# Weight rows of 512 columns kept even columns first, odd ones behind, and read back in turn

## The chip, the core and the metric

The kernel runs on one core of one Trainium2 chip, as one program in one launch. The metric is the device time of one execution in microseconds (us). TensorE is called PE in the profile, its loading of the stationary operand PEld, VectorE is DVE, ScalarE is ACT, GpSimd POOL, and SP is the engine that issues most DMAs.

## What is computed

The reference is a trunk of two layers over one sequence of 256 tokens with 1024 channels, in float32. Cut to what matters here:

```python
def _token_mixer(xn, w_in, w_pool, pool_scale, w_a, w_b, w_o, rel_bias):
    u, q, k, v, g_pool, g_attn = jnp.split(xn @ w_in, SPLITS, axis=-1)
    ...
    merged = jax.nn.sigmoid(g_pool) * (pool_out @ w_a) + jax.nn.sigmoid(g_attn) * (attn_out @ w_b)
    return merged @ w_o

def _conv_ffn(xn, w_up, conv_w, conv_b, w_down):
    a, gval = jnp.split(xn @ w_up, 2, axis=-1)
    a = lax.conv_general_dilated(a, conv_w[:, None, :], ...) + conv_b
    return (jax.nn.gelu(a) * gval) @ w_down

def reference(x, ...):
    h = x
    for layer in range(DEPTH):
        h = h + _token_mixer(_rmsnorm(h, norm1[layer]), w_in[layer], ...)
        h = h + _conv_ffn(_rmsnorm(h, norm2[layer]), w_up[layer], ...)
    return _rmsnorm(h, norm_f)
```

Nearly all arithmetic is in the products with the weights `w_in` (1024 x 7680 a layer), `w_a`, `w_b`, `w_o`, `w_up` (1024 x 5632) and `w_down` (2816 x 1024). Each weight is used for 256 tokens only, so all of them pass from memory through the chip once.

## The kernel before, in words

**Two parts of every number.** The matrix unit is fed with float32r operands, which keep fewer bits than float32. So each float32 number is split into a high part (float32r) and a low part (what is left). A product of activations with weights is then three products: high with high, high with low, low with high, all added up in one PSUM tile.

**Weights.** The class `Weights` streams them. A load is one DMA of 1 MB from SP into a tile `raw` of 128 partitions x 2048 columns of float32 (three such buffers). A load is cut into two pieces of 128 x 1024 columns. For each piece, `open_next` gives two instructions: ACT copies the piece into `wh` with a cast to float32r (L191), and DVE subtracts that copy from the raw piece and writes `wl` (L192). There are five buffers each of `wh` and `wl` (some pieces use other tiles: `m2`, `ybig`, `at2`, `v1`), and the splitting runs three or more pieces ahead of the products. In the first layer's first eight pieces the split also multiplies by the norm's gain, 512 columns at a time (L199 on ACT, L200 on DVE).

**Products by rows.** Here the activations are the stationary operand (128 channels x 128 tokens, loaded into the array), and the weights stream past as the moving operand, 512 columns wide, into a PSUM tile of 128 tokens x 512 output columns. Three helpers do this:

- `v_sum` (called by `by_rows` and for the values): six products of a weight piece that holds two rows of 512 columns (L667). It serves `w_in`, `w_a`, `w_b` and `w_up`.
- `residual_mm` with its inner function `one` and `row_mm` (L564, L565, L566): weight pieces of one row of 1024 columns, read in slices of 512 columns, and near the end of a layer in some slices of 256. It serves `w_o` and `w_down`.
- `product` in `values_of_x` (L789): the first 96 products of the first layer.

**Products by channels.** For some queries and keys (`proj`, L536 and L538) and for the pool projections (`chunk_mm`, L528 to L530) the weights are the stationary operand and the activations move. These pieces have rows of 128 or 256 columns.

**Order.** The program runs in one stream on PE; every stage waits only for its piece of weights and for the activations of the stage before. The vector engines split weights ahead of PE, and between the splits they take results out of PSUM, build the attention's softmax, the convolution and the gelu. Every `wh` and `wl` buffer is handed back when the products that read it are done; ACT's next cast into that buffer waits for that.

The changed functions, and what calls them:

Of the kernel before, what the change touches and what calls it, by code (L numbers as in the profile page):

```python
# [75 lines left out]
def _edge_table():  # L76

    rows = []
    for w in WINDOWS:
        h = w // 2  # L80
        left = [w / (i + h) for i in range(h)]
        right = [w / (S - i + h) for i in range(S - h + 1, S)]
        rows.append(left + right + [1.0] * (16 - w + 1))
    return np.asarray(rows, np.float32).reshape(1, 64)


class Weights:
# [82 lines left out]
    def open_next(self):  # L170


        nc, i = self.nc, self.n_split
        n, cut, shape, slot = self.pieces[i]
        if slot is None:
            self.live.add(i)
            h, l = (
                self.pool.tile([P, *shape], F32R, tag=tag, bufs=self.BUFS, name=f"{tag}{i}")
                for tag in ("wh", "wl")
            )  # L180
        else:
            tag, part, of = (*slot, 0, 1)[:3]
            if part == 0:
                self.shared = self.idle.tile([P, of, 2, *shape], F32R, tag=tag, name=f"{tag}{i}")
            h, l = self.shared[:, part, 0], self.shared[:, part, 1]
        src = cut(self.raw[n])
        self.split[i] = (h, l)
        self.n_split += 1
        if i >= self.n_scaled:
            return [(  # L190
                lambda: nc.scalar.copy(out=h, in_=src),  # L191
                lambda: nc.vector.tensor_sub(out=l, in0=src, in1=h.bitcast(F32)),  # L192
            )]

        def scaled(j):
            k = i // 2 * shape[0] + j
            g = self.gains[:, k : k + 1]
            return (
                lambda: nc.scalar.activation(h[:, j], src[:, j], AF.Copy, scale=g),  # L199
                lambda: nc.vector.scalar_tensor_tensor(  # L200
                    out=l[:, j], in0=src[:, j], scalar=g, in1=h[:, j].bitcast(F32),
                    op0=ALU.mult, op1=ALU.subtract,
                ),
            )

        return [scaled(j) for j in range(shape[0])]
# [15 lines left out]
def encoder(ctx, tc, x, w_in, w_pool, pool_scale, w_a, w_b, w_o, norm1, norm2, w_up, conv_w,  # L222
# [20 lines left out]
    def rows(w, r0, n=2, c0=0, width=1024, tag=None, pieces=2):  # L243

        src = w[r0 : r0 + n * P, c0 : c0 + width].rearrange("(k p) c -> p k c", p=P)
        h = n // pieces
        return W.add(
            src, (n, width), [((lambda t, j=j: t[:, j * h : (j + 1) * h, :]), (h, width)) for j in range(pieces)],
            tag,
        )  # L250

    for l in range(DEPTH):
        if l == 0:
            slots = (("m2", 0, 2), ("m2", 1, 2), ("ybig",), ("at2",))
            for j in range(2):
                kept = rows(w_in[l], j * 512, 4, C_V, 512)
# [18 lines left out]
        for c in PAIRS:  # L275
            q = cols(w_in[l], C_Q + c * 256)
            k = cols(w_in[l], C_K + c * 256)
# [19 lines left out]
        for kind, n in ORDER.split():  # L297
            n = int(n)
# [4 lines left out]
            for j in range(2):  # L303
                if kind == "d":
                    W.use(rows(w_down[l], (4 * n + 2 * j) * P))
                elif kind == "r":
                    src = w_up[l][j * 512 : (j + 1) * 512].rearrange("(k p) c -> p k c", p=P)
                    c0 = (4 * n * P, 4 * n * P + DFF)
# [9 lines left out]
                else:  # L318
                    p = rows(w_up[l], j * 512, 4, (kind == "g") * DFF + 4 * n * P, 512)
# [4 lines left out]
    h = const.tile([P, 2, D], F32, name="h")  # L324
# [195 lines left out]
    def flush():  # L520

        while later:
            later.pop(0)()
# [38 lines left out]
    def row_mm(ps, ah, al, wh, wl, first, last):  # L562

        nc.tensor.matmul(ps, ah, wh, start=first, stop=False)  # L564
        nc.tensor.matmul(ps, ah, wl, start=False, stop=False)  # L565
        nc.tensor.matmul(ps, al, wh, start=False, stop=last)  # L566

    def residual_mm(parts, n, done, hold=4, fill=None, ahead=0, seeded=False):

        ps = [[acc.tile([P, 512], F32, tag="acc", name="res_ps") for _ in range(2)] for _ in range(2)]

        def one(part, ps_, t, cc, start, stop):
            ah, al, wh, wl = part
            row_mm(ps_, ah[:, t], al[:, t], wh[:, 0, cc], wl[:, 0, cc], start, stop)

        held = []
        for k in range(n):  # L580
            ah, al = parts(k)
            i, (wh, wl) = W.get(W.LOOK + ahead * (k >= n - hold - 2))
            flush()
            part = (ah, al, wh, wl)
            if k < n - hold:
                for t in range(2):
                    for c in range(2):
                        one(part, ps[t][c], t, slice(c * 512, c * 512 + 512), k == 0, False)
                W.free(i)
            else:  # L590
                held.append((i, part))
            yield
        then, half = None, None
        seed = None
        if seeded:
            one_r = sm.tile([P, P], F32R, tag="u", name="one_r")
            nc.scalar.copy(out=one_r, in_=ident)
        for t in range(2):
            segments = SEGMENTS[t]
            if t and seeded:  # L600
                segments = segments[1], segments[0], segments[2]
            for m, cc in enumerate(segments):
                c, c0 = divmod(cc.start, 512)
                res = ps[t][c][:, c0 : c0 + cc.stop - cc.start]
                if c0:

                    if not seed:
                        nc.vector.tensor_add(out=h[:, t, cc], in0=res, in1=h[:, t, cc])
                    res = mmp.tile([P, cc.stop - cc.start], F32, tag="mm", name="res2_ps")
                for j, (i, part) in enumerate(held):  # L610
                    one(part, res, t, cc, c0 != 0 and j == 0, j == hold - 1)
                    if c0 and j == 1:
                        for more in seed or ():
                            nc.tensor.matmul(res, one_r, more, start=False, stop=False)
                if half:
                    run(half)
                    half = None
                if then and m:
                    half = then()
                    next(half)  # L620
                    then = None
                then = done(t, m, cc, res, c0 != 0 and seeded) or then
                if t and seeded and m == 0:
                    rest = slice(768, D)
                    hi, lo = seed = [sm.tile([P, 256], F32R, tag="us", name="seed") for _ in range(2)]
                    nc.vector.tensor_add(out=h[:, t, rest], in0=ps[t][1][:, 256:], in1=h[:, t, rest])
                    nc.scalar.copy(out=hi, in_=h[:, t, rest])
                    nc.vector.tensor_sub(out=lo, in0=h[:, t, rest], in1=hi.bitcast(F32))
        if half:
            run(half)  # L630
        rest = fill() if fill else None
        half = then()
        next(half)
        if rest:
            rest()
        run(half)
        for i, _ in held:
            W.free(i)

    def run(gen):  # L640
        for _ in gen:
            pass
# [16 lines left out]
    def v_tile():  # L659
        return acc.tile([P, 512], F32, tag="acc", name="v_ps")  # L660

    def v_sum(ps, x2, t, n, piece, of=4):

        _, (wh, wl) = piece
        passes = [(0, wh, 0), (0, wl, 0), (1, wh, 0), (0, wh, 1), (0, wl, 1), (1, wh, 1)]
        for m, (part, w, j) in enumerate(passes):
            nc.tensor.matmul(  # L667
                ps, x2[:, 2 * n + j, part, t, :], w[:, j, :], start=(n + m == 0),
                stop=(n == of - 1 and m == 5),
            )  # L670

# [48 lines left out]
    def values_of_x(keep_values):  # L720
# [49 lines left out]
        x2 = two_parts("x", "x2")  # L770
        ps = [[v_tile() for _ in range(2)] for _ in range(2)]
# [14 lines left out]
        def product(k, g, t, kind):  # L786
            wh, wl = W.split[pieces[k // 2 * 2, g]]
            a, w = {"hh": (xuh, wh), "lh": (xul, wh), "hl": (xuh, wl)}[kind]
            return nc.tensor.matmul(  # L789
                ps[g][t], a[:, k, t, :], w[:, k % 2, :], start=k == 0 and kind == "hh",  # L790
                stop=k == KD - 1 and kind == "hl",
            )

# [110 lines left out]
    for l in range(DEPTH):  # L904
# [21 lines left out]
        if l == 0:  # L926
            with tc.manual_schedule():
                x2 = values_of_x(keep_values)
        else:
            for g in range(2):  # L930
                held = begun[0] if g == 0 else [W.get() for _ in range(4)]
                for t in range(2):
                    if g + t == 0:
                        ps = begun[1]
                    else:
                        ps = v_tile()
# [264 lines left out]
        for c in PAIRS:  # L1201
            for n in range(4):
                src, rest = (halves(a) for a in proj(x2))
# [27 lines left out]
        ps = by_rows(x2, 4, step)  # L1231
# [14 lines left out]
        for n, cc in enumerate(HALVES):  # L1246
            ps = by_rows(x2, 4, step)
# [67 lines left out]
        x2 = two_parts("x", "x2")  # L1315
# [150 lines left out]
        for kind, n in ORDER.split():  # L1466
# [9 lines left out]
            if (kind, n) == ("a", "0"):  # L1476
                held, ps = entry
                ps = [ps, v_tile()]
# [6 lines left out]
            else:  # L1485
                ps = by_rows(x2, 4, unit, W.LOOK + 1)
            n = int(n)
# [3 lines left out]
        if l + 1 < DEPTH:  # L1491
            x2 = two_parts("x", "x2")
# [34 lines left out]
```

## Time and profile before

| what | value |
|---|---|
| time, median of three runs | 857.28 us (857.15 to 857.35) |
| the profiled execution's own time | 857.48 us |
| its span, first to last instruction | 855.7 us |
| granted PE clock, mean | 0.999 |
| PE busy | 848.6 us, 4030 products |
| PEld busy | 711.5 us |
| DVE busy | 648.8 us |
| ACT busy | 477.3 us |
| POOL busy | 20.7 us |
| read from HBM | 160.65 MB |

The durations of products in the profile overlap: a product of 512 columns is listed with about 389 ns, but the next one starts long before those are over, and the ends are modelled. How long PE really takes for a product is therefore read from the distance between starts, as a stretch of the chain or of the timeline shows it. "f32" in a product's row is the size of its operands; they are float32r where the code says so. Names such as `rows_ps<-wh,x` give the output tile and the two inputs.

### The profile page before, as it was taken

The page shows a single profiled execution, that of the slowest core. Times are in us where ns is not written, and L with a number is a line of the kernel's source. Part 1 is how long each engine was busy: PE and PEld are TensorE (multiplying, and loading weights), DVE is VectorE, ACT ScalarE, POOL GpSimd, SP SyncE. Part 2 cuts the span into 40 slices and gives each one's busy share as a digit, 9 for nine tenths or more (in the row PEclk, how much of TensorE's full clock was granted, in tenths as well). Part 3 has the DMA queues.
Part 4 walks back from the last instruction along what each step waited for, and adds up shares of the span by engine and source line. Part 5 has one row for each costly group of instructions (what it writes and reads, how often), then busy time and mean ns, then how long its engine had stood idle before and what let it go on. Part 6 is the DMA issues. An engine that isn't in the chain of part 4 may idle for free.

```text
span 855.7 us, 11282 instructions
## 1 busy us (share of the span) xinstructions
PE 848.6 (99%) x4030; PEld 711.5 (83%) x4030; DVE 648.8 (76%) x918; ACT 477.3 (56%) x700; POOL 20.7 (2%) x55
## 2 busy tenths in 40 slices
PE   9999999999999999999999999999999999999997
PEld 7888888888888888888888889888888888888886
DVE  6967889566767789899556597886567757999974
ACT  7735465444545566767444445654445436767762
POOL 1120000000010000000000000000000000000001
PEclk9999999999999999999999999999999999999999
DMA  8787684764846777777526665658659276777751
GB/s 314 235 261 249 192 264 163 225 226 131 310 173 223 234 237 243 249 241 270 197 99 207 230 222 185 238 175 244 200 201 315 107 219 203 243 243 244 253 183 50
DMA packets 101308, 186.07 MB, mean 217 GB/s; under 512 B 9774, under 2 KB 28414, under 8 KB 101252
## 3 DMA queue, kind: packets, MB, share of 16 engines
q1 hardware_dynamic: 100388, 183.71, 64.9%
q0 software_dynamic: 560, 1.33, 0.6%
q8 instruction: 32, 0.52, 0.3%
q10 hardware_dynamic: 304, 0.30, 0.1%
q14 instruction: 24, 0.20, 0.1%
HBM read 160.65 MB, written 1.59 MB: 190 GB/s over the span
## 4 chain that ended last, share of the span: by engine, by line
PE 99%; DMA 0%; SPq 0%; POOLq 0%; issue 0%; ACT 0%; DVEq 0%; DVE 0%; POOL 0%; ACTq 0%
PE rows_ps L667 61%; PE res_ps L566 6%; PE res_ps L565 6%; PE res_ps L564 6%; PE v_ps L667 5%; PE proj_ps L536 3%; PE v_ps L789 3%; PE proj_ps L538 2%; PE s_ps L1077 1%; PE o_ps L1152 1%; PE s_ps L1072 1%; PE o_ps L1148 1%; PE xt_ps L495 1%; PE pool_ps L530 0%; PE pool_ps L529 0%; PE pool_ps L528 0%
## 5 line engine op out<-in xcount | busy, mean ns | idle before, releaser
L192 DVE TENSOR_TENSOR wl<-raw,wh 128x1024 fp32r<-128x1024 f32 x278 | 336.8, 1217 | 149.8 <-ACT wh L191 146.0
L667 PE MATMUL rows_ps<-wh,x 128*128 128x512 f32 x1344 | 420.0, 391 | 0.0
L191 ACT CAST wh<-raw 128x1024 fp32r<-128x1024 f32 x278 | 289.1, 1049 | 210.9 <-PE rows_ps L667 121.9
L667 PEld LDWEIGHTS rows_ps<-wh,x 128*128 128x128 f32 x1344 | 252.3, 188 | 52.2
L667 PE MATMUL rows_ps<-wl,x 128*128 128x512 f32 x672 | 261.5, 389 | 0.0
L667 PEld LDWEIGHTS rows_ps<-wl,x 128*128 128x128 f32 x672 | 126.2, 188 | 25.6
L564 PE MATMUL res_ps<-wh,actq 128*128 128x512 f32 (+1 forms) x152 | 57.5, 378 | 0.0
L565 PE MATMUL res_ps<-wl,actq 128*128 128x512 f32 (+1 forms) x152 | 57.4, 378 | 0.0
L566 PE MATMUL res_ps<-wh,actk 128*128 128x512 f32 (+1 forms) x152 | 57.4, 378 | 0.0
L667 PE MATMUL rows_ps<-wh,po 128*128 128x512 f32 x128 | 41.2, 393 | 0.0
L564 PEld LDWEIGHTS res_ps<-wh,actq 128*128 128x128 f32 x152 | 28.6, 188 | 5.4
L565 PEld LDWEIGHTS res_ps<-wl,actq 128*128 128x128 f32 x152 | 28.6, 188 | 5.4
L566 PEld LDWEIGHTS res_ps<-wh,actk 128*128 128x128 f32 x152 | 28.6, 188 | 5.3
L536 PE MATMUL proj_ps<-x,wh 128*128 128x512 f32 x128 | 32.2, 393 | 0.0
L702 DVE STREAM_TRANSPOSE up_rows<-rows_ps 128x512 f32<-128x512 f32 x40 | 26.3, 692 | 3.1 <-PE rows_ps L667 3.1
L667 PEld LDWEIGHTS rows_ps<-wh,po 128*128 128x128 f32 x128 | 24.0, 188 | 4.9
L1394 ACT ACTIVATE yg<-a,prm 128x256 f32<-128x256 f32 x44 | 26.5, 602 | 1.4
L564 PE MATMUL res_ps<-wh,m 128*128 128x512 f32 (+1 forms) x72 | 26.7, 371 | 0.0
L536 PEld LDWEIGHTS proj_ps<-x,wh 128*128 128x128 f32 x128 | 23.1, 189 | 4.2
L566 PE MATMUL res_ps<-wh,m 128*128 128x512 f32 (+1 forms) x72 | 26.5, 368 | 0.0
L565 PE MATMUL res_ps<-wl,m 128*128 128x512 f32 (+1 forms) x72 | 26.3, 366 | 0.0
L464 ACT ACTIVATE junk<-h 128x512 f32<-128x512 f32 (+1 forms) x19 | 10.5, 552 | 28.1 <-DVE h L462 28.1
(226 smaller groups left out, 1049.4 us busy)
## 6 DMA issues: line engine op xcount, KB each, us to landing
raw<-in_w_in_dram SPq DMA_DIRECT2D x56, 1024.0 KB, 5.8
raw<-in_w_up_dram SPq DMA_DIRECT2D x40, 1024.0 KB, 6.0
raw<-in_w_down_dram SPq DMA_DIRECT2D x22, 1024.0 KB, 5.5
up_turned<-up_rows SPq DMA_DIRECT2D x160, 64.0 KB, 3.8
raw<-in_w_a_dram SPq DMA_DIRECT2D x8, 1024.0 KB, 4.8
raw<-in_w_o_dram SPq DMA_DIRECT2D x8, 1024.0 KB, 8.9
qk<-qk_rows SPq DMA_DIRECT2D x64, 64.0 KB, 2.2
pt<-rows SPq DMA_DIRECT2D x64, 64.0 KB, 3.8
```

The source lines that it names most:

```text
L191: lambda: nc.scalar.copy(out=h, in_=src),
L192: lambda: nc.vector.tensor_sub(out=l, in0=src, in1=h.bitcast(F32)),
L464: nc.scalar.activation(junk, new, AF.Square, scale=D**-0.5, accum_out=ss[:, n : n + 1])
L536: nc.tensor.matmul(ps, wh(k), x2[:, k], start=(k == 0), stop=False)
L538: nc.tensor.matmul(ps[:, 1], wl(k), x2[:, k, 0], start=False, stop=(k == nk - 1))
L564: nc.tensor.matmul(ps, ah, wh, start=first, stop=False)
L565: nc.tensor.matmul(ps, ah, wl, start=False, stop=False)
L566: nc.tensor.matmul(ps, al, wh, start=False, stop=last)
L667: nc.tensor.matmul(ps, x2[:, 2 * n + j, part, t, :], w[:, j, :], start=(n + m == 0), stop=(n == of - 1 and m == 5),)
L702: nc.vector.transpose(out=out[:, :, t].rearrange("p j c r -> p c j r"), in_=ps[t].rearrange("p (c j r) -> p c j r", c=4, j=4),)
L789: return nc.tensor.matmul(ps[g][t], a[:, k, t, :], w[:, k % 2, :], start=k == 0 and kind == "hh", stop=k == KD - 1 and kind == "hl",)
L1394: nc.scalar.activation(y, aj, AF.Identity, bias=b, scale=w1)
```

## The change

Three helper functions are new. `in_turn` views the raw piece so that, within each block of 512 columns, the 256 even columns come first and the 256 odd ones behind. ACT's cast and DVE's subtraction read the raw piece through this view, so they read every second float32 (a step of 8 bytes), first the even and then the odd ones. They write `wh` and `wl` without gaps, as before (`kept` only gives the output the same shape). Where a row is no multiple of 512 columns (the pieces of the products by channels), nothing changes.

`moving` is the view through which the products by rows read `wh` and `wl`: first column 0 of the even half, then column 0 of the odd half, 256 places (1 KB) further, then back to column 1 of the even half, and so on. The columns so reach the array in the order in which they stood in the raw weights, and the output is the same columns in the same order. Of the three helpers above, all products by rows read in this way, those of 256 columns too.

No instruction is added or left out, and the instructions of each engine stand in the same order as before. DMAs, buffers and waits are the same. Only the places that ACT and DVE read, and that PE reads as the moving operand, are others.

```diff
+def in_turn(a):
+
+    if a.shape[-1] % 512:
+        return a
+    return a.rearrange("p k (c b a) -> p k c a b", a=2, b=256)
+
+
+def kept(a):
+    if a.shape[-1] % 512:
+        return a
+    return a.rearrange("p k (c a b) -> p k c a b", a=2, b=256)
+
+
+def moving(w, j, cc):
+
+    c, c0 = divmod(cc.start, 512)
+    n = cc.stop - cc.start
+    w = w[:, j, c * 512 : c * 512 + 512].rearrange("p (a b) -> p b a", a=2)
+    return w[:, c0 // 2 : (c0 + n) // 2, :]
...
-        src = cut(self.raw[n])
+        src = in_turn(cut(self.raw[n]))
         self.split[i] = (h, l)
         self.n_split += 1
+        h, l = kept(h), kept(l)
...
-            row_mm(ps_, ah[:, t], al[:, t], wh[:, 0, cc], wl[:, 0, cc], start, stop)
+            row_mm(ps_, ah[:, t], al[:, t], moving(wh, 0, cc), moving(wl, 0, cc), start, stop)
...
-                ps, x2[:, 2 * n + j, part, t, :], w[:, j, :], start=(n + m == 0),
+                ps, x2[:, 2 * n + j, part, t, :], moving(w, j, slice(0, 512)), start=(n + m == 0),
...
-                ps[g][t], a[:, k, t, :], w[:, k % 2, :], start=k == 0 and kind == "hh",
+                ps[g][t], a[:, k, t, :], moving(w, k % 2, slice(0, 512)), start=k == 0 and kind == "hh",
```

## The prediction

> **What bounds the kernel now.** I read the page's busy times first, then the chain of work that ended last, then PE's waits. The busy times, as microseconds and share of the span:
>
> ```profile
> PE 848.6 (99%) x4030; PEld 711.5 (83%) x4030; DVE 648.8 (76%) x918; ACT 477.3 (56%) x700; POOL 20.7 (2%) x55
> ```
>
> The chain, by engine and by line, and all of PE's waits of the execution (in total, times, longest):
>
> ```profile
> PE 99%; DMA 0%; SPq 0%; POOLq 0%; issue 0%; ACT 0%; DVEq 0%; DVE 0%; POOL 0%; ACTq 0%
> ...
> PE gain_ps L377 <- DVE mhalf L366: 1.0, 1, 1.0
> PE xt_ps L737 <- DMA h<-in_x_dram: 0.4, 1, 0.4
> ```
>
> PE is the chain. It idles for 855.7 - 848.6 = 7.1 us, nearly all before the first and after the last product, and waits for others 1.4 us. A busy PE could still be one that starts its products late, so I took the distance between starts from two stretches without gaps: one piece of the chain with 240 products of 512 columns (start, length), and a stretch of the timeline with products of 256 columns, 0.12 us apart.
>
> ```profile
> 41.33 54.42 PE rows_ps L667 x240
> ...
> 98.36 0.28 PE L528 MATMUL pool_ps<-plh,wh 128*128 128x256 f32 x1
> 98.48 0.28 PE L529 MATMUL pool_ps<-pll,wh 128*128 128x256 f32 x1
> ...
> 99.68 0.28 PE L530 MATMUL pool_ps<-plh,wl 128*128 128x256 f32 x1
> ```
>
> 54.42 / 240 = 226.7 ns for 512 columns; (99.68 - 98.36) / 11 = 120 ns for 256. The difference, 106.7 ns for 256 columns, is 0.417 ns a column; what is left, 226.7 - 512 x 0.417 = 13.3 ns, is a fixed part of each product. So PE takes in a column of the moving operand every 0.417 ns without a pause, and the span is the sum of columns and fixed parts. A change to how fast columns arrive at PE is paid in full; a change on ACT or DVE is paid only when they fall behind.
>
> **Which products the change touches.** The counts by line, from the busy times of one line in two stretches, the second one the rest of the span (two rows of L667, then one of L789, which has no product later), and from the line's own view (L564; L565 and L566 are its equals in `row_mm`, three products a call):
>
> ```profile
> 0.00:428.00 428.00, 277.02 (x1200) 1.00 0.70 232
> 428.00:856.00 428.00, 298.58 (x1296) 1.00 0.61 203
> ...
> 0.00:428.00 428.00, 23.39 (x96) 1.00 0.70 232
> ...
> L564 PE MATMUL res_ps<-wh,actq x152: 277/389/396, 368.6 to 849.7; 128*128 128x512 f32 x136, 128*128 128x256 f32 x16
> L564 PE MATMUL res_ps<-wh,m x72: 278/389/487, 224.0 to 668.3; 128*128 128x512 f32 x56, 128*128 128x256 f32 x16
> L564 PE MATMUL res_ps<-wh,actv x32: 389/389/390, 401.2 to 832.6; 128*128 128x512 f32 x32
> ```
>
> L667 has 1200 + 1296 = 2496 products, all of 512 columns. L564 to L566 have 3 x (136 + 56 + 32) = 672 of 512 and 3 x (16 + 16) = 96 of 256. With the 96 of L789, all of 512, that is 3264 products of 512 and 96 of 256 columns. They take 3264 x 226.7 + 96 x 120 ns = 751.5 of the 855.7 us. Of that, 3264 x 213.3 + 96 x 106.7 ns = 706.5 us is the streaming of columns, which is what the change puts at stake.
>
> **Part 1, the split on ACT and DVE.** Both now read the raw piece with a step of two words. Both engines already do just this in `pool`, where tokens are taken with a step of two (L989 on ACT, L990 on DVE); beside them stand rows of the same size that read without a step (L809, L810). Columns: busy, mean ns of one, idle before.
>
> ```profile
> L989 ACT CAST plh<-pd 128x512 fp32r<-128x512 f32 x8 | 5.3, 666 | 12.6 <-DVE u L958 10.2 <-DVE pd L982 2.5
> L809 ACT CAST x<-xu 128x512 fp32r<-128x512 f32 x4 | 2.5, 616 | 1.0 <-DVE xu L804 1.0
> ...
> L990 DVE TENSOR_TENSOR pll<-pd,plh 128x512 fp32r<-128x512 f32 x8 | 5.5, 685 | 0.0
> ...
> L810 DVE TENSOR_TENSOR x<-xu,x 128x512 fp32r<-128x512 f32 x4 | 2.7, 683 | 0.5 <-ACT x L809 0.5
> ...
> L191 ACT CAST wh<-raw 128x1024 fp32r<-128x1024 f32 x278 | 289.1, 1049 | 210.9 <-PE rows_ps L667 121.9 <-DMA raw<-in_w_up_dram 24.1 <-PE res_ps L566 19.6
> ...
> L192 DVE TENSOR_TENSOR wl<-raw,wh 128x1024 fp32r<-128x1024 f32 x278 | 336.8, 1217 | 149.8 <-ACT wh L191 146.0 <-DMA up_turned<-up_rows 1.5 <-DMA u<-u 1.5
> ```
>
> ACT: 666 - 616 = 50 ns for 512 columns, so 100 ns for a piece of 1024: L191 goes from 1049 to about 1149, 278 x 0.1 = 28 us more busy time on an engine that is busy 56%. The cover is L191's own idle time, 121.9 us of it waiting for PE's products of L667 to free a buffer. DVE: 685 against 683, nothing. Both at 0 us on the path. Were the cover gone, the bound is these 28 us. Only the first eight pieces, split in halves of 512 columns in the first 30 us, lie close to PE: 16 x 50 ns, at most 0.8 us.
>
> A rule speaks against this part. The Trainium skill, Vector Engine (DVE) Microarchitecture Reference, section "Measured stream behaviour on trn2 (trn3 not measured)", says that a port keeps its full rate only in runs of two or more adjacent 4-byte words, and lists 1.73 instead of 1.054 ns a column where one source hops at every element. By that table DVE's split would grow by an estimated 0.69 us a piece and DVE to about 847 us, as much as the span. The row of L990 is the same operation with a step of two words and shows none of it, so I go by the row.
>
> **Part 2, PE's reading.** No product of the trace reads its moving operand with a jump at every column, so its price has to be bounded. Below: nothing (0.417 ns a column stays), and less than nothing only if the fixed 13.3 ns were due to the way of reading; 3360 x 13.3 ns = 45 us would be the most, 812.8 us. Above, by other engines' rates for one word after the other: L809 and L191 give ACT's (1049 - 616) / 512 = 0.846 ns a column, L810 and L192 DVE's (1217 - 683) / 512 = 1.043 ns. The dearest row of 512 columns read from SBUF, its fixed part included, is ACT's exponential:
>
> ```profile
> L1098 ACT ACTIVATE probs<-probs,nm 128x512 f32<-128x512 f32 x16 | 11.5, 721 | 7.2 <-DVE nm L1088 7.1
> ```
>
> That is 1.41 ns a column. I take the doubling, 0.833 ns, as nearest to ACT's row: PE takes two adjacent words in the time in which ACT takes one (0.417 against 0.846), so it must get two words from one place at each beat; from the changed layout each place gives one, and the beat stays. Each product of 512 columns then costs 226.7 + 213.3 = 440 ns, each of 256 columns 226.7 ns. Sum: 3264 x 213.3 + 96 x 106.7 ns = 696.3 + 10.2 = 706.5 us. Nothing covers it, since PE is the chain; PEld (about 188 ns a load, under the products) gains cover, and ACT, DVE and the DMAs get almost twice the time for the same work, so none of them becomes late.
>
> The rule that fits this row is in the Trainium skill, SBUF — State Buffer, section "Specifications (TRN2)": lines of 16 bytes, at least two hits in a line for full bandwidth, a penalty at each step to a new line. Before, each line serves four columns; after, each read goes to another line than the one before. Read as half the rate it gives the same sum, an estimate of 1564 us; no product before reads like this, so the trace cannot agree or disagree.
>
> **The sum.** The profiled execution's own time is 857.48 us, span 855.7 and 1.8 around it, 0.2 us above the median of three runs, 857.28. 857.5 + 706.5 + 0 (ACT, DVE) = 1564 us.
>
> **Rivals.**
>
> *PE's reader keeps both places open.* It returns to the same two places in turn, so if it holds what it fetched from both, columns go on at 0.417 ns and nothing moves but ACT's covered 28 us: 857.5 us, at most 858.3 with the start's 0.8. It decides if a second fetched place survives one read of another. For it: L990, where skipping every second word is free, and a stream without a gap over 240 products, as if fetched ahead. Against it: PE needs words 2.5 times as fast as DVE (1.043 / 0.417), so a reserve on DVE need not be one on PE. The same Trainium skill section on DVE streams notes one read stream that alternated between two regions at the full read rate, which would be this rival; no row here shows it. Chance 0.25 within 0.2%, and 0.02 for a gain by the fixed part.
>
> *A part of the price.* Fetching ahead hides half: 0.625 ns a column, 857.5 + 353 = 1211 us. It decides if jumps cost, but less than the time that a pair takes. Nothing in the rows speaks for one value between 865 and 1450. Chance 0.12, with a trifle over 0.2% from the start's split included.
>
> *DVE's rate.* At 1.043 ns a column: 0.626 x (3264 x 512 + 96 x 256) ns = 1062 us more, 1920 us. Against it: PE reads nothing else at that rate. Chance 0.07.
>
> *Each jump waits for its fetch.* The price is then above one word a beat; with 1.41 ns a column 857.5 + 1684 = 2542 us, and if one column costs what four cost now (1.667 ns) 857.5 + 2120 = 2977 us. It decides if fetches of unconnected places do not overlap. For it: ACT loses 50 ns on 512 columns in L989 merely by a step of two words, so it has little reserve for unconnected reads. Chance 0.18.
>
> *The change does nothing,* since the view is folded back into a plain one: excluded, as the order in which columns leave a permuted buffer must be permuted too.
>
> **How the numbers follow.** The forecast, 1564 us, has 0.36 (1450 to 1650). Its bounds come from a little cover at the start and from ACT's 0.846 ns (1585 us). The range leaves out the rival that waits for each fetch (0.18) and the gain (0.02): from 855 us, no change, to 1930 us, just over DVE's rate. About 0.2%, 1.7 us, is what a measurement of this kernel can tell from no change. Faster by more: 0.02. Within: 0.25. Slower: 0.36 + 0.12 + 0.07 + 0.18 = 0.73.
>
> **What would show it.** Right: a run of 240 such products takes 240 x 0.44 = 105.6 us in the chain instead of 54.42; products by channels stay at 120 ns for 256 columns; PE stays near 99% busy while DVE and ACT fall to about half of their shares; ACT's cast near 1149 and DVE's subtraction near 1217 ns. Wrong: 226.7 ns between starts (the reader holds both places), over 540 ns (each fetch waits), or a PE that idles for `wl` (DVE pays for the step after all, its split far over 1217 ns).

## The result, and the profile after

The changed kernel takes 866.14 us (median of 4 runs, 863.6 to 868.56) against 857.21 us before (4 runs): ratio 1.0104, 95% interval 1.0074 to 1.0133. It is slower, by 1%, where 82% were forecast. The profiled execution took 863.60 us, with a span of 861.8.

First the page's busy times:

```profile
PE 827.8 (96%) x4030; PEld 716.0 (83%) x4030; DVE 727.2 (84%) x918; ACT 610.2 (71%) x700; POOL 20.5 (2%) x55
```

PE's busy time fell by 20.8 us, while it now idles for 861.8 - 827.8 = 34 us. ACT is busy for 133 us more and DVE for 78 us more, with the same instructions. Now the starts of six products of 512 columns in the first layer, before and after (start, duration, line):

```profile
13.27 0.39 PE L789 MATMUL v_ps<-wh,xuh 128*128 128x512 f32 x1
...
14.40 0.39 PE L789 MATMUL v_ps<-wl,xuh 128*128 128x512 f32 x1
```

```profile
13.05 0.38 PE L811 MATMUL v_ps<-wh,xuh 128*128 128x512 f32 x1
...
14.13 0.38 PE L811 MATMUL v_ps<-wl,xuh 128*128 128x512 f32 x1
```

Five steps take 1.13 us before and 1.08 after: 226 and 216 ns a product. The median distance between starts, over all products by rows of 512 columns, is 227 ns before and 216 after (both traces' starts, in whole ns). So reading in turn did not make a product dearer; it made it about 11 ns cheaper. The split did the opposite. These are the groups that answer to those of before, and three that the change does not touch; two of the three are shown from before first, and the third, L989, stands in the prediction (busy, mean ns of one, idle before):

```profile
L1394 ACT ACTIVATE yg<-a,prm 128x256 f32<-128x256 f32 x44 | 26.5, 602 | 1.4
L1393 ACT COPY a<-up_turned 128x256 f32<-128x256 f32 x44 | 18.3, 415 | 2.7 <-DMA up_turned<-up_rows 2.7
```

```profile
L213 ACT CAST wh<-raw 128x1024 fp32r<-128x1024 f32 x278 | 413.7, 1512 | 100.3 <-PE rows_ps L689 42.6 <-DMA raw<-in_w_in_dram 16.4 <-DMA raw<-in_w_up_dram 13.5
L1416 ACT ACTIVATE yg<-a,prm 128x256 f32<-128x256 f32 x44 | 26.4, 601 | 1.4
L1415 ACT COPY a<-up_turned 128x256 f32<-128x256 f32 x44 | 23.2, 526 | 0.4 <-DMA up_turned<-up_rows 0.4
...
L1011 ACT CAST plh<-pd 128x512 fp32r<-128x512 f32 x8 | 6.9, 859 | 16.6 <-DVE u L980 14.1 <-DVE pd L1004 2.5
...
L214 DVE TENSOR_TENSOR wl<-raw,wh 128x1024 fp32r<-128x1024 f32 x278 | 408.3, 1478 | 92.9 <-ACT wh L213 91.2
```

ACT's cast takes 1512 ns instead of 1049 (1149 was forecast), DVE's subtraction 1478 instead of 1217 (1217 was forecast). L1011 is the pool's cast from which the price was taken (L989 before): the same instruction, with the same operands, went from 666 to 859 ns. L1415, which writes with a step of two words, went from 415 to 526. L1416, which neither reads nor writes with a step, stayed at 601 (602 before). So something slows accesses to SBUF with a step of two words; among the groups of ACT and DVE that take over 1.5 us in all, none without such a step grew by more than about 3%. The eight pool casts of the changed kernel show it within one execution: the six that run beside PE's reading in turn (L689) take 855 to 1022 ns, the two that run beside products by channels 675 and 680. PE's waits show where it is paid (in total, times, longest):

```profile
PE res_ps L587 <- DVE wl L214: 6.0, 14, 1.2
PE mt_ps L1366 <- DVE th L1294: 5.5, 2, 2.8
PE rows_ps L689 <- DVE wl L214: 5.4, 7, 0.9
```

Before there were two waits of 1.4 us in all. PE now waits for `wl` in many places, and for other results of DVE.

### The profile page after: what moved, and what is told of

The parts are those of the page before. It is cut to its first block, busy times and chain, and to the rows that moved or that the text cites. A ratio compares the mean times of both kernels' runs of the same rounds, so it can differ in the third digit from the quotient of the medians.

```text
span 861.8 us, 11282 instructions
## 1 busy us (share of the span) xinstructions
PE 827.8 (96%) x4030; PEld 716.0 (83%) x4030; DVE 727.2 (84%) x918; ACT 610.2 (71%) x700; POOL 20.5 (2%) x55
## 5 line engine op out<-in xcount | busy, mean ns | idle before, releaser
L214 DVE TENSOR_TENSOR wl<-raw,wh 128x1024 fp32r<-128x1024 f32 x278 | 408.3, 1478 | 92.9 <-ACT wh L213 91.2
L213 ACT CAST wh<-raw 128x1024 fp32r<-128x1024 f32 x278 | 413.7, 1512 | 100.3 <-PE rows_ps L689 42.6
L689 PE MATMUL rows_ps<-wh,x 128*128 128x512 f32 x1344 | 405.7, 380 | 2.0 <-DVE xu L826 2.0
L689 PEld LDWEIGHTS rows_ps<-wh,x 128*128 128x128 f32 x1344 | 254.1, 189 | 37.9 <-issue 2.4
L689 PE MATMUL rows_ps<-wl,x 128*128 128x512 f32 x672 | 255.9, 381 | 5.5 <-DVE wl L214 5.4
L689 PEld LDWEIGHTS rows_ps<-wl,x 128*128 128x128 f32 x672 | 127.0, 189 | 27.2 <-DVE wl L214 9.9
L689 PE MATMUL rows_ps<-wh,po 128*128 128x512 f32 x128 | 39.7, 382 | 0.0
L1416 ACT ACTIVATE yg<-a,prm 128x256 f32<-128x256 f32 x44 | 26.4, 601 | 1.4
L689 PEld LDWEIGHTS rows_ps<-wh,po 128*128 128x128 f32 x128 | 24.2, 189 | 3.3
L1435 ACT ACTIVATE y<-y 128x512 f32<-128x512 f32 x22 | 13.9, 632 | 17.7 <-DVE y L1430 17.5
```

What stands on the lines that cost most here:

```text
L689: nc.tensor.matmul(ps, x2[:, 2 * n + j, part, t, :], moving(w, j, slice(0, 512)), start=(n + m == 0), stop=(n == of - 1 and m == 5),)
L1416: nc.scalar.activation(y, aj, AF.Identity, bias=b, scale=w1)
L1435: nc.scalar.activation(y2, y2, AF.Tanh, scale=c)
```

## The experiments

The theory after this comparison (A): PE's reading in turn makes a product 11 ns cheaper, and it slows accesses with a step of two words on ACT and DVE beside it; the split, which has just such accesses, then starves PE. The first rival (B): the step costs that much in the split by itself. The second (C): a PE that is 5% faster cannot be fed by this split at all.

**Only PE reads in turn.** Weights are split and stored as before the change.

```diff
+def moving(w):
+    return w.rearrange("p (a b) -> p b a", a=2)
...
-                ps, x2[:, 2 * n + j, part, t, :], w[:, j, :], start=(n + m == 0),
+                ps, x2[:, 2 * n + j, part, t, :], moving(w[:, j, :]), start=(n + m == 0),
```

The same is done in `residual_mm` and `product`.

> Only the reading of PE is changed: weights are split and stored as before, without a step, and the products by rows read column 0, then column 256, then column 1 and so on; the output's columns so come out in another order than the reference's. In the changed kernel these products stand 215.7 ns apart instead of 226.7, but PE idles for the split, whose rows grew from 1049 to 1512 ns on ACT and from 1217 to 1478 on DVE. Theory A (PE's reading in turn slows what reads or writes every second word on ACT and DVE, and only that): products 215.7 ns apart, split at 1049 and 1217 ns, time 857.3 - 3264 x 11 ns = about 821 us; the pool's cast with a step of two words, which is in all these kernels, stays near 860 ns as in the changed kernel (666 before). Theory B (the step alone costs that much in the split, whatever PE reads): also about 821 us, but the pool's cast back at 666 ns. Theory C (the split cannot feed a PE that is 5% faster, with or without a step): over 835 us, with PE waiting for wl.

Measured: 826.34 us (825.93 to 828.87), ratio 0.9647, interval 0.9631 to 0.9664. The starts stand 216 ns apart. The split and the pool's cast:

```profile
L195 ACT CAST wh<-raw 128x1024 fp32r<-128x1024 f32 x278 | 286.6, 1043 | 176.4 <-PE rows_ps L671 86.8 <-DMA raw<-in_w_up_dram 27.5 <-DMA raw<-in_w_in_dram 23.9
...
L993 ACT CAST plh<-pd 128x512 fp32r<-128x512 f32 x8 | 6.6, 825 | 14.8 <-DVE u L962 12.4 <-DVE pd L986 2.5
...
L196 DVE TENSOR_TENSOR wl<-raw,wh 128x1024 fp32r<-128x1024 f32 x278 | 336.1, 1217 | 124.1 <-ACT wh L195 122.5
```

The split without a step is as fast as before, and the pool's cast, with a step that it always had, is as slow as in the changed kernel. B and C fall: B wanted 666 ns for the cast, C over 835 us. Of the 36 us that 3264 products could save, 31 arrive; PE's waits in this trace come to 5.0 us instead of 1.4, 2.5 of them for `wl` at L569, the second of `row_mm`'s three products.

**Only the split is changed.** The splitting reads with a step as in the changed kernel; the products read the stored rows straight through.

```diff
-                ps, x2[:, 2 * n + j, part, t, :], moving(w, j, slice(0, 512)), start=(n + m == 0),
+                ps, x2[:, 2 * n + j, part, t, :], w[:, j, :], start=(n + m == 0),
```

(against the changed kernel, and likewise in `residual_mm` and `product`).

> Only the split is changed: ACT and DVE read every second column as in the changed kernel and store even columns first, but the products by rows read the stored rows straight through; the products so use columns in another order than the reference's. Theory A (the split is slow only beside a PE that reads in turn): ACT's cast about 1150 ns as forecast, DVE's subtraction 1217, products 226.7 ns apart, time 857 to 859 us. Theory B (the step alone): 1512 and 1478 ns also here, PE waits for wl as in the changed kernel, and with products of 226.7 ns the time is 866 us or more.

Measured: 857.34 us (10 runs, 856.99 to 858.69), ratio 1.0001, interval 0.9992 to 1.0011.

```profile
L213 ACT CAST wh<-raw 128x1024 fp32r<-128x1024 f32 x278 | 308.8, 1120 | 196.1 <-PE rows_ps L689 118.5 <-DMA raw<-in_w_up_dram 23.0 <-PE res_ps L588 15.7
...
L214 DVE TENSOR_TENSOR wl<-raw,wh 128x1024 fp32r<-128x1024 f32 x278 | 337.1, 1218 | 145.3 <-ACT wh L213 141.4 <-DMA u<-u 1.5 <-DMA up_turned<-up_rows 1.5
```

The cast at 1120 ns and the subtraction at 1218 are Part 1 of the prediction to a few per cent, and they cost nothing. The two halves of the change cost nothing and save 31 us when they stand alone; together they lose 9. That is an interaction, and theory A says which.

**Writing in turn instead of reading with a step.** The same stored order, made by reading the raw piece straight and writing to both halves in turn.

```diff
-    return a.rearrange("p k (c b a) -> p k c a b", a=2, b=256)
+    return a.rearrange("p k (c b a) -> p k c b a", a=2, b=256)
...
-    return a.rearrange("p k (c a b) -> p k c a b", a=2, b=256)
+    return a.rearrange("p k (c a b) -> p k c b a", a=2, b=256)
```

> The same stored order and the same reading by PE as in the changed kernel, but the split reads the raw piece straight through and writes in turn into the even and the odd half, 1 KB apart, instead of reading every second word; DVE reads ACT's copy in turn too. If only reading with a step of two words is slowed beside PE (theory A in its narrow form), ACT's cast is near 1049 and DVE's subtraction near 1217 ns and the time about 821 us. If every place that is used for one word at a time costs, as in the changed kernel or more, the rows are at 1500 ns or above and the time is 866 us or above.

Measured: 981.51 us, ratio 1.144 (1.1419 to 1.146), with ACT's cast at 2186 and DVE's subtraction at 2137 ns:

```profile
L213 ACT CAST wh<-raw 128x1024 fp32r<-128x1024 f32 x278 | 567.3, 2186 | 50.3 <-DMA raw<-in_w_in_dram 13.5 <-PE rows_ps L689 9.8 <-DMA raw<-in_w_up_dram 8.9
```

The time is on the side of the second expectation. How much of the 2186 ns is the jump itself and how much comes from PE was not separated, so this kernel alone does not refute the narrow form, in which only reads suffer beside PE; L1415 does, which reads runs of adjacent words, writes with a step, and went from 415 to 526 ns in the changed kernel. Here accesses without a step are slower too: the cast of `x` (L831, L809 before) takes 816 ns instead of 616, and ACT's tanh of `pa` 754 instead of 599. In the other kernels the two stay at 616 to 635 and 593 to 601 ns.

**Which engine's step costs.** From the kernel in which only PE reads in turn, one of the two engines gets the step back; `in_turn` and `kept` are those of the change.

```diff
-                lambda: nc.scalar.copy(out=h, in_=src),
+                lambda: nc.scalar.copy(out=kept(h), in_=in_turn(src)),
```

```diff
-                lambda: nc.vector.tensor_sub(out=l, in0=src, in1=h.bitcast(F32)),
+                lambda: nc.vector.tensor_sub(out=kept(l), in0=in_turn(src), in1=kept(h).bitcast(F32)),
```

> As the kernel in which only PE's reading was changed (826.3 us), but ACT's cast reads every second column while DVE's subtraction reads straight through, so that the low parts do not belong to the high parts. If ACT's slower cast is what starves PE in the changed kernel: cast about 1500 ns, subtraction 1217, time 855 to 866 us. If it is DVE's: 826 to 840 us.

> As the kernel in which only PE's reading was changed, but DVE's subtraction reads the raw piece with a step of two words while ACT's cast reads straight through, so that the low parts do not belong to the high parts. If DVE's slower subtraction is what starves PE in the changed kernel: subtraction about 1480 ns, cast 1049, time 850 to 866 us. If it is ACT's: 826 to 835 us. If both are needed, this one and the one with ACT's step lie both well under 860.

Measured: ACT's step alone 849.32 us (846.92 to 851.66; cast 1489, subtraction 1219 ns), DVE's alone 845.47 us (843.57 to 847.3; cast 1043, subtraction 1487 ns). Against 826.34 that is 23.0 and 19.1 us, in sum 42.1, where both together cost 866.14 - 826.34 = 39.8. Neither engine is "the" cause: each piece of weights goes through the cast, then the subtraction, then the product, and a longer stay on either delays it.

**What reading patterns cost PE.** Two kernels, each run once, give a pattern of its own to each of `v_sum`'s four weight pieces and to each product of `row_mm`. In the first, runs of r adjacent columns are taken from the two halves in turn; in the second, single columns from `a` places.

```diff
+    return w.rearrange("p (a b r) -> p b a r", a=2, r=r)
...
+    return w.rearrange("p (a b) -> p b a", a=a)
```

> Split and storage as before; each kind of product by rows reads its row of 512 columns in another pattern, each on a line of its own, so that the output's columns come out in another order than the reference's. Runs of r adjacent columns are taken from the two halves in turn: v_sum's four weight pieces with r = 256 (the two halves swapped: one jump), 1, 8 and 2, row_mm's three products with r = 4, 16 and 64, the first layer's first products with r = 128. Theory D (what is saved is a fixed part at a product's start that any reading in more than one piece avoids): 215.7 ns between starts for every r. Theory E (what is saved comes from taking consecutive columns from two places): 215.7 ns for r = 1, 226.7 for long runs, with a border somewhere between 2 and 16.

> Split and storage as before; each kind of product by rows takes one column from each of a places in turn, a and the distance between the places being 2 and 256 words (the first layer's first products), 4 and 128, 8 and 64, 16 and 32, 256 and 2 (v_sum's four pieces), 64 and 8, 128 and 4, 32 and 16 (row_mm's three products); the output's columns come in another order than the reference's. Theory F (what counts is that consecutive columns come from different places, however many): about 216 ns between starts for all distances of 4 words and more. Theory G (two places are kept open and more thrash): 216 ns for a = 2 alone, and 240 to 440 ns for larger a, 8 ns up or more.

The times, 938.03 and 1475.83 us, are mixtures. The chain, in order of time, shows the patterns apart; each piece is 12 products (start, length, line). The runs: L682 has r = 2, L676 the two halves swapped (one jump), L678 r = 1:

```profile
300.76 4.08 PE rows_ps L682 x12
304.83 2.75 PE rows_ps L676 x12
307.58 2.59 PE rows_ps L678 x12
```

A product takes 340 ns for r = 2, 243 for r = 8 (L680, 2.92 us for the 12 that follow), 229 for one jump (227 by the median of starts, as before) and 216 for r = 1. Neither D (a fixed part that any two pieces avoid) nor E (a border with long runs at 226.7) holds: runs of 2 to 64 columns are dearer than plain reading, and only single columns are cheaper. The places: L673 has 4 places 128 words apart, L675 8 places, L677 16, and L679 reads with a plain step of two words:

```profile
531.99 3.39 PE rows_ps L673 x12
535.38 5.88 PE rows_ps L675 x12
541.26 5.20 PE rows_ps L677 x12
546.46 5.41 PE rows_ps L679 x12
```

283, 490, 433 and 451 ns. The first layer's products, with two places, stand 216 ns apart in this kernel too. Theory G holds in the main (490 lies above its 440): two places are served at 216 ns, more are not. A price near the doubling that was forecast (440 ns) is there for 8 places or more and for the plain step, but not for the pattern that the change uses. One thing more shows in these kernels. While PE read from 4 places 128 words apart or from 16 places, the pool's cast took 683 ns in the mean. And in the kernel of runs, ACT's copies of `u`, which write with a step of two words, took 490 to 549 ns beside r = 1 and 424 to 448 beside r = 2, which comes from the same two halves. It is not any odd reading by PE that slows the steps elsewhere.

**How far apart the two places are.** One run: the two places are 64, 32, 16 and 8 words apart in `v_sum`, 4, 2 and 128 in `row_mm`.

```diff
+    return w.rearrange("p (x a b) -> p x b a", a=2, b=d)
```

> Split and storage as before; products by rows take columns from two places in turn, with the distance between the places being 64, 32, 16 and 8 words (v_sum's four pieces), 4, 2 and 128 words (row_mm's three products), and moving on to the next block after twice that; the output's columns come in another order than the reference's. If any two places are kept open, all distances of 4 words and more give about 216 ns, with little added per block. If the distance matters (the places must lie in different parts of the memory), short distances give 240 to 450 ns, as a plain step of two words did (451).

The time was 829.27 us. All distances but 2 words give 216 ns (medians of starts); 2 words, as an order 0, 2, 1, 3 within four adjacent columns, gives 235. So the border is as expected, but the steps on ACT were a surprise. These are two pairs of equal copies with a step of two words (256 columns each), the first beside products whose places are 16 words apart (L677), the second beside 64 (L673):

```profile
67.48 0.38 PE L677 MATMUL rows_ps<-wh,x 128*128 128x512 f32 x1
67.57 0.74 ACT L969 COPY u<-u 128x256 f32<-128x256 f32 x2 [1.43 <-DMA u<-u]
...
73.43 0.89 ACT L969 COPY u<-u 128x256 f32<-128x256 f32 x2
73.53 0.38 PE L673 MATMUL rows_ps<-wl,x 128*128 128x512 f32 x1
```

0.74 against 0.89 us for the pair. So theory A needs a term: the steps suffer when PE takes single columns from two places that lie far apart. Two kernels tested that on the change itself, with blocks of 16 or 128 columns kept even first instead of 512 (the first eight pieces stay as in the change):

```diff
-    return a.rearrange("p k (c b a) -> p k c a b", a=2, b=256)
+    return a.rearrange("p k (c b a) -> p k c a b", a=2, b=d)
...
+    return w[:, j, cc].rearrange("p (c a b) -> p c b a", a=2, b=d)
```

> The changed kernel with blocks of 16 columns instead of 512: the 8 even columns first, the 8 odd ones behind, so that PE takes columns in turn from places 8 words apart (the first eight pieces keep blocks of 512). The split still reads with a step of two words. The output is the reference's. Where PE read from places 4 to 128 words apart, products stood 215.7 ns apart too, but the pool's cast with a step of two words took 709 ns (666 beside plain reading, 825 to 859 beside places 256 words apart). Theory H (the split is slowed by how far apart PE's two places are): ACT's cast 1100 to 1200, DVE's subtraction 1220 to 1270 ns, time 826 to 832 us. Theory A without distance (any reading in turn slows it): about 1500 and 1480 ns, 862 to 868 us.

> As the kernel with blocks of 16 columns, but with blocks of 128: PE's places are 64 words apart. Theory H in a gradual form: ACT's cast between that of blocks of 16 and the changed kernel's 1512 ns, time between. Theory H with a border: equal to blocks of 16 (826 to 832 us) if the border lies above 64 words, equal to the changed kernel (862 to 868 us) if below.

Measured: blocks of 16 give 830.29 us (828.8 to 832.46), ratio 0.9695 (0.9678 to 0.9711); blocks of 128 give 866.40 us (866.0 to 871.41), ratio 1.0121 (1.0093 to 1.0149). The split and the pool's cast in the one and in the other:

```profile
L218 ACT CAST wh<-raw 128x1024 fp32r<-128x1024 f32 x278 | 315.1, 1147 | 165.4 <-PE rows_ps L694 82.9 <-DMA raw<-in_w_up_dram 27.2 <-DMA raw<-in_w_in_dram 16.8
...
L1016 ACT CAST plh<-pd 128x512 fp32r<-128x512 f32 x8 | 5.4, 670 | 15.2 <-DVE u L985 12.7 <-DVE pd L1009 2.5
...
L219 DVE TENSOR_TENSOR wl<-raw,wh 128x1024 fp32r<-128x1024 f32 x278 | 336.2, 1218 | 127.6 <-ACT wh L218 125.3
```

```profile
L218 ACT CAST wh<-raw 128x1024 fp32r<-128x1024 f32 x278 | 412.6, 1510 | 99.5 <-PE rows_ps L694 42.9 <-DMA raw<-in_w_in_dram 17.8 <-DMA raw<-in_w_up_dram 17.2
...
L1016 ACT CAST plh<-pd 128x512 fp32r<-128x512 f32 x8 | 6.8, 847 | 16.5 <-DVE u L985 14.0 <-DVE pd L1009 2.5
...
L219 DVE TENSOR_TENSOR wl<-raw,wh 128x1024 fp32r<-128x1024 f32 x278 | 407.6, 1475 | 96.7 <-ACT wh L218 95.4
```

Same stored kind of order, same step in the split, same 216 ns a product: with places 8 words apart the split is as fast as beside plain reading (1147 and 1218), with 64 words apart as slow as in the changed kernel. The block size also changes the order in which the split itself reads, but the pool's cast, which is the same instruction in all these kernels, goes with it: 670 against 847 ns. So it is PE's reading that decides. There is a border, not a slope. In the kernel of mixed distances the copies beside 8, 16 and 32 words took 0.41 to 0.45 us each and those beside 64 words alone 0.48 to 0.60 (from the trace's single instructions), so it lies between 32 and 64 words.

**Versions that beat both.** Besides the blocks of 16, the stored order can be left alone and the order undone where PSUM is read. In the first of two kernels `v_sum` and `product` read in turn and their readers of PSUM use a view; in the second `row_mm` and the residual sums do so too, in blocks of 256.

```diff
+def in_columns(ps):
+    return ps.rearrange("p (b a) -> p a b", a=2)
...
-            nc.scalar.activation(pa[0][:, t, cc], ps[t], AF.Tanh, scale=0.5)
+            nc.scalar.activation(by_half(pa[0][:, t, cc]), in_columns(ps[t]), AF.Tanh, scale=0.5)
```

> Split and storage as in the kernel before. The products by rows of v_sum and of the first layer read columns 0, 256, 1, 257 and so on; the order that this leaves in PSUM is undone by those who read PSUM (DVE's block transposes, ACT's tanh and value copies, DVE's gate products), through a view with a step of two words; the two projections of row_mm read straight through. The output is the reference's. If PSUM reads with a step of two words cost little beside PE's reading in turn, 2592 products come 11 ns sooner: 857.3 - 28.5 = about 829 us, up to 834 with stalls like those of the kernel in which only PE's reading was changed (826.3 where 821 was expected). If these reads are slowed like the split's (a third or more), the 72 or so reads per layer lie on the path of the stages and the time is 840 us or more.

> As the kernel whose readers of PSUM undo the order (831.5 us), but the projections of row_mm read in turn too, from places 128 words apart within blocks of 256 columns, and the residual sums read PSUM through a view with a step of two words. The output is the reference's. If two places 128 words apart serve as well as two 256 apart, 672 more products of 512 columns come 11 ns sooner and 96 of 256 columns some 8 ns: 831.5 - 8.2 = about 823 us; the reads of PSUM by the residual sums, which the norms wait for, may give back 1 us. If the jump from block to block matters, row_mm stays at 226 ns or goes above, and the time is 831 us or more.

Measured: 831.51 us (829.75 to 832.47), ratio 0.9699 (0.9684 to 0.9713), and 826.53 us (824.89 to 828.51), ratio 0.9649 (0.9635 to 0.9663). The reads of PSUM with a step cost nothing that shows in the first of the two: the block transposes stay at 693 ns (692 before, L702), the tanh of `pa` at 593 (599 before, L1244). With the blocks of 16 these are three versions that are 3.0 to 3.5% faster than the kernel before.

```profile
L1257 ACT ACTIVATE pa<-rows_ps 128x512 f32<-128x512 f32 x8 | 4.6, 593 | 3.7 <-PE rows_ps L679 3.7
```

## Why the prediction was wrong

**What bounds the kernel: right.** PE was the chain, and a gain in the distance between products came through: 3264 products x 11 ns is 36 us, and 31 us were measured where only this was changed.

**Part 2, PE's reading: wrong.** The step that failed is "from the changed layout each place gives one, and the beat stays". It put 706.5 us into the sum; the term is worth -31 us. The doubling exists (431 to 490 ns a product with 8 or more places or with a plain step, 440 forecast) but not for two places in turn. The rival "PE's reader keeps both places open" is what the runs bear out in effect (no run shows what the reader holds), and I gave it 0.25. Its number was wrong too, since it left the fixed 13.3 ns of a product alone. That the fixed part could be due to the way of reading was priced, as the bound below (812.8 us), and got 0.02: of the 13.3 ns, 216 - 213.3 = 2.7 are left. The Trainium skill, TensorE: Matmul & The Clock Gate, section "Back-to-back issue gap", gives N / 2.4 + 2.5 ns as the gap of an isolated product of N columns, about 216 ns for 512. Plain reading of these operands does not reach it here (226.7), reading in turn does, and the 131 ns that the same section gives for a sustained stream is reached by no run here. Why plain reading costs 11 ns more is open.

Of the two rules weighed, the one in the Trainium skill, SBUF — State Buffer, section "Specifications (TRN2)", on lines of 16 bytes, does not describe PE here: two places 1 KB apart change the line at each read and cost nothing, while a plain step of two words, with two reads in each line, takes 451 ns. The note in the Trainium skill, Vector Engine (DVE) Microarchitecture Reference, section "Measured stream behaviour on trn2 (trn3 not measured)", that a DVE stream alternating between two regions was read at the full rate, is like what PE did; it stood beside the rival that I ranked second.

One row of Part 2 was misread. The dearest row of 512 columns read from SBUF is not ACT's exponential (721 ns) but DVE's scaled subtraction at L200 (748 ns). That would move the rival in which each jump waits from 2542 to about 2630 us, and nothing else.

**Part 1, the split: right where it was measured, wrong where it was used.** Its rows came from a program in which PE reads plainly. Beside plain reading the forecast holds (1149 forecast, 1120 measured; 1217 and 1218). Beside PE reading from places 64 or 256 words apart it does not: 1512 and 1478. "Both at 0 us on the path" became 40 us, by the two kernels with one step each about half from either engine. I had set the rule against DVE's step aside by the row of L990; the subtraction took 1.22 us a piece beside plain reading and 1.48 in the changed kernel. The rule in the Trainium skill, Vector Engine (DVE) Microarchitecture Reference, the same section, gave an estimated 1.9 us.

**The direction: right by luck.** The forecast said slower because of PE; it is slower because of ACT and DVE, in spite of PE. The range held 866 us only because it reached down to the rival. The sum that the runs give: 857.2 - 31 (PE) + 40 (split) = 866.

**Open.** What ACT, DVE and PE share that makes steps of two words slow when PE's places are 64 or more words apart, and free at 32 or fewer, was not tried. Nor was the whole of why the kernel with PE's part alone saves 31 and not 36 us: 3.6 us more of waits on PE are in its trace, and its own steps of two words (825 instead of 666 ns in the pool, 520 instead of 415 in the convolution) are slow too, but no run took them away alone.

## What to carry to other kernels

A price read from a row holds beside what ran at that time: if the change alters what another engine reads at the same moment, the row of an unchanged instruction before and after is the first thing to compare. Two changes that are each harmless or good alone can lose together, so run each alone before judging the pair. And where a product's fixed part has no explanation, the way its operand is read is a suspect worth one run: here it was 3.5% of the kernel, at no cost in instructions.

## What the runs showed of the hardware

- A product of 512 float32r columns takes 226.7 ns from start to start when the moving operand is read plainly, and 216 when single columns are read in turn from two places 4 to 256 words apart. With 4 places it takes 283 ns, with 8 or more or with a step of two words 431 to 490, and with runs of two columns from two places 340.
- While PE reads single columns in turn from two places 64 or 256 words apart, ACT's and DVE's accesses to SBUF with a step of two words are slower: 1510 against 1147 ns (ACT, 1024 columns read), 1475 against 1218 (DVE), 526 against 415 (ACT, 256 columns written). In the changed kernel accesses without a step are not (601 and 602 ns), and with places 8 words apart none is. The border lies between 32 and 64 words: copies with a step took 0.41 to 0.45 us beside places 8, 16 and 32 words apart and 0.48 to 0.60 beside 64.
- Reads of PSUM with a step of two words by DVE's block transposes and ACT's tanh took what they took without a step (693 and 593 ns).
